# A FiLM layer on one core: loads moved to one queue and cut shorter, stores made longer

## The chip, the cores and the metric

The kernel runs on one core of a Trainium2 chip. The metric is the device time of one execution in microseconds (us), as the median of several runs. A core has a matrix engine (TensorE, PE in the profile), a vector engine (VectorE, DVE), a scalar engine (ScalarE, ACT), a general-purpose vector engine (GpSimd, POOL) and a synchronisation engine (SyncE, SP). They run side by side and wait for one another by semaphores. Data moves between the chip's main memory (DRAM) and the on-chip memory (SBUF, 128 partitions) by 16 DMA engines. A DMA is issued by an engine's instruction queue; here SP and ACT issue them, and each has a queue of its own at every DMA engine (q1 is SP's and q10 is ACT's in this profile). PSUM is the small memory into which TensorE writes.

## The reference

A batch of 32 sequences, each 512 rows of 256 numbers, is scaled and shifted column by column. The scale and the shift depend on the batch entry, and come from two small matrix products. All is float32.

```python
batch, seq, dim = 32, 512, 256      # x: (32, 512, 256); cond_dim = 64
gamma = conditioning @ gamma_proj   # (32, 64) @ (64, 256)
beta = conditioning @ beta_proj
return x * (1 + gamma[:, None, :]) + beta[:, None, :]
```

x is 16.78 MB and so is the output. The small inputs are 8 KB (conditioning) and 64 KB each (the two projections).

## The kernel before, in words

x is cut into four slabs of 8 batch entries (4.19 MB each). In a slab, each of the 128 partitions holds 32 consecutive rows of 256 numbers, which is 32 KB in one piece of DRAM; 16 partitions hold one batch entry. All four slabs have buffers of their own (tiles `xs`), so no load ever waits for a buffer.

**Loads.** SP issues all loads of x at the start (line 59): slab 0 in two DMAs of 8 and 24 rows per partition (runs of 8 and 24 KB), the others in one DMA each (runs of 32 KB). ACT issues the three small loads (lines 48 to 51). A DMA of 128 partitions is dealt out over the 16 DMA engines, 8 partitions to each; a DMA engine moves one run per packet, and adds a small packet that signals completion.

**Preparation.** GpSimd builds a 32 by 32 identity, which VectorE spreads to 32 by 512 (line 67), each column 16 times. One matrix product with it transposes the conditioning and repeats each batch entry 16 times (line 72), so that a column stands for a partition; VectorE copies the result to SBUF (line 74). For each slab a second product (line 79) gives gamma and beta for its 128 partitions, side by side in PSUM (`gb_p`). ScalarE copies them to SBUF (`gb_s`), adding 1 to gamma on the way (lines 82 and 85).

**Work on the slabs.** A slab is worked off in two groups of 16 rows per partition. Of a group VectorE takes 11 rows: it multiplies by (gamma + 1) (line 100) and adds beta (line 103), reading gamma and beta from PSUM. GpSimd takes the other 5 rows with the copies in SBUF (lines 102 and 104). When both are done, ACT issues the store of the group (line 105): 16 rows per partition, runs of 16 KB, 2.1 MB, eight stores in all. The order in which a queue takes its instructions comes from the Tile scheduler's own planning; on GpSimd it came out as two multiplications, then two additions. The scheduler also gives each DMA one of eight semaphores in turn, so a later DMA is issued only when an earlier holder of its semaphore has landed.

Of the kernel before, what the change touches and what calls it, by code (L numbers as in the profile page):

```python
# [2 lines left out]

# [5 lines left out]


@with_exitstack
def kernel(
    ctx: ExitStack,
    tc: tile.TileContext,
    x: bass.AP,
    conditioning: bass.AP,
    gamma_proj: bass.AP,
    beta_proj: bass.AP,
    out: bass.AP,  # L20
):
    nc = tc.nc
    f32 = mybir.dt.float32
    ALU = mybir.AluOpType

    batch, seq, dim = x.shape
    cond_dim = conditioning.shape[1]
    P = 128
    SLABS = 4
    BS = batch // SLABS  # L30
    REP = P // BS
    ROWS = BS * seq // P
    assert SLABS * BS == batch and REP * BS == P and ROWS * REP == seq

    x_v = x.flatten_outer_dims().rearrange("(s p r) d -> s p r d", s=SLABS, p=P)
    o_v = out.flatten_outer_dims().rearrange("(s p r) d -> s p r d", s=SLABS, p=P)

    LOADS = {0: [8, 24]}
    GROUP = 16
    ON_DVE = 11  # L40

    consts = ctx.enter_context(tc.tile_pool(name="consts", bufs=1))
    xpool = ctx.enter_context(tc.tile_pool(name="xpool", bufs=1))
    psum = ctx.enter_context(tc.tile_pool(name="psum", bufs=1, space=bass.MemoryType.PSUM))


    cond_s = consts.tile([batch, cond_dim], f32)
    nc.scalar.dma_start(out=cond_s, in_=conditioning)  # L48
    gbproj = consts.tile([cond_dim, 2 * dim], f32)
    nc.scalar.dma_start(out=gbproj[:, :dim], in_=gamma_proj)  # L50
    nc.scalar.dma_start(out=gbproj[:, dim:], in_=beta_proj)

    slabs = []
    for s in range(SLABS):
        xs = xpool.tile([P, ROWS, dim], f32, name=f"xs{s}")
        slabs.append(xs)
        r = 0
        for n in LOADS.get(s, [ROWS]):
            nc.sync.dma_start(out=xs[:, r : r + n, :], in_=x_v[s, :, r : r + n, :])
            r += n  # L60
        assert r == ROWS


    ident = consts.tile([batch, batch], f32)
    make_identity(nc, ident)
    rident = consts.tile([batch, batch * REP], f32)
    nc.vector.tensor_copy(  # L67
        out=rident.rearrange("p (b g) -> p b g", g=REP),
        in_=ident.to_broadcast([batch, batch, REP]),
    )  # L70
    cond_T_p = psum.tile([cond_dim, batch * REP], f32)
    nc.tensor.matmul(cond_T_p, lhsT=cond_s, rhs=rident, start=True, stop=True)  # L72
    cond_T = consts.tile([cond_dim, batch * REP], f32)
    nc.vector.tensor_copy(out=cond_T, in_=cond_T_p)  # L74

    gb_p, gb_s = [], []
    for s in range(SLABS):
        p_t = psum.tile([P, 2 * dim], f32, name=f"gb_p{s}")
        nc.tensor.matmul(p_t, lhsT=cond_T[:, s * P : (s + 1) * P], rhs=gbproj,  # L79
                         start=True, stop=True)  # L80
        s_t = consts.tile([P, 2 * dim], f32, name=f"gb_s{s}")
        nc.scalar.activation(out=s_t[:, :dim], in_=p_t[:, :dim],  # L82
                             func=mybir.ActivationFunctionType.Identity,
                             bias=1.0, scale=1.0)
        nc.scalar.copy(out=s_t[:, dim:], in_=p_t[:, dim:])  # L85
        gb_p.append(p_t)
        gb_s.append(s_t)

    def rows(t, n):
        return bass.AP(tensor=t.tensor, offset=t.offset, ap=[t.ap[0], [0, n], t.ap[1]])  # L90

    for s in range(SLABS):
        xs = slabs[s]
        g_p, b_p = gb_p[s][:, :dim], gb_p[s][:, dim:]
        g_s, b_s = gb_s[s][:, :dim], gb_s[s][:, dim:]
        for r0 in range(0, ROWS, GROUP):
            v = xs[:, r0 : r0 + ON_DVE, :]
            w = xs[:, r0 + ON_DVE : r0 + GROUP, :]
            nv, nw = ON_DVE, GROUP - ON_DVE
            nc.vector.scalar_tensor_tensor(out=v, in0=rows(g_p, nv), scalar=1.0, in1=v,  # L100
                                           op0=ALU.add, op1=ALU.mult)
            nc.gpsimd.tensor_tensor(out=w, in0=w, in1=rows(g_s, nw), op=ALU.mult)  # L102
            nc.vector.tensor_add(out=v, in0=v, in1=rows(b_p, nv))  # L103
            nc.gpsimd.tensor_tensor(out=w, in0=w, in1=rows(b_s, nw), op=ALU.add)  # L104
            nc.scalar.dma_start(out=o_v[s, :, r0 : r0 + GROUP, :],
                                in_=xs[:, r0 : r0 + GROUP, :])


# [1 line left out]
_INS = ['x', 'conditioning', 'gamma_proj', 'beta_proj']  # L110
_OUTS = [((32, 512, 256), 'float32')]


# [23 lines left out]
```

## Time and profile before

| what | value |
|---|---|
| median of five runs | 84.65 us (84.44 to 84.71) |
| the profiled execution | 84.44 us |
| its span, from first to last instruction | 82.7 us |
| VectorE busy | 49.9 us (60%) |
| GpSimd busy | 46.2 us (56%) |
| TensorE busy | 9.1 us (11%) |
| DMA, both queues | 96.5% of 16 engines' span |
| moved | 33.69 MB, 408 GB/s over the span |
| VectorE works on slabs | from 17.61 to 66.7 us |
| last store issued | 66.77 us |

The span begins with the first instruction of the program and ends with its last; the 1.7 us between it and the execution's time lie outside the program's instructions. The page gives the busy time of each engine, then the span in 40 slices with a digit for tenths, then the DMA queues with the share of 16 engines' time that their packets took. A row of the busy times by stage gives the stretch (start and end in us), its length, the busy time of PE, PEld (weight loads), DVE, ACT and POOL with counts of instructions, TensorE's granted clock (1.00 throughout), the DMA engines' share and GB/s. Packets are counted at their start there, so a short stretch with long packets can show a share above or below what was really used. A row of the timeline gives start, duration, engine, line, operation, the tiles written and read, their shapes, and in brackets the idle time before it and what ended it. A row of the issues gives what is written and read, the queue, how many, KB each, and the median time from issue to landing.

### The profile page before, as it was taken

To read this page: it belongs to the slowest core of one execution; us is meant where nothing else is said; L and a number is where in the kernel's file an instruction comes from. 1 tells how busy PE (TensorE), PEld (TensorE's weight loads), DVE (VectorE), ACT (ScalarE), POOL (GpSimd) and SP (SyncE) were. 2 spreads that over 40 slices of the span, in tenths; PEclk is the share of its full clock that TensorE was granted. 3 is DMA by queue.
4 is the path that set the end of the run, shared out by engine and by line. 5 is a ranking of instruction groups with operands and counts; after the bars stand their busy time and mean duration, and the time that the engine had idled before them with its cause. 6 is when DMAs were issued, how large, how long until landed. Compare 5 with 4: busy or idle time off the path is not lost.

```text
span 82.7 us, 156 instructions
## 1 busy us (share of the span) xinstructions
PE 9.1 (11%) x10; PEld 2.8 (3%) x10; DVE 49.9 (60%) x18; ACT 3.9 (5%) x9; POOL 46.2 (56%) x22
## 2 busy tenths in 40 slices
PE   0090000899600000000000000000000000000000
PEld 0010000443000000000000000000000000000000
DVE  2002000049999999999999999999999920000000
ACT  0600000034400000000000000000000000000000
POOL 2000000059999999999999999999995000000000
DMA  3799999969969989998989969999999999999992
GB/s 56 317 527 396 389 396 523 460 301 507 507 301 460 507 365 381 412 476 381 396 381 523 476 293 476 389 452 436 404 476 389 452 436 404 476 389 452 436 404 103
DMA packets 2080, 33.69 MB, mean 408 GB/s; under 512 B 288, under 2 KB 416, under 8 KB 416
## 3 DMA queue, kind: packets, MB, share of 16 engines
q1 hardware_dynamic: 720, 16.78, 48.6%
q10 hardware_dynamic: 1360, 16.92, 47.9%
HBM read 16.92 MB, written 16.78 MB: 408 GB/s over the span
## 4 chain that ended last, share of the span: by engine, by line
DVE 48%; DMA 16%; issue 11%; PE 2%; ACTq 1%; ACT 1%
DVE xs L100 30%; DVE xs L103 19%; DMA gbproj<-in_beta_proj_dram 16%; PE gb_p L79 2%; ACTq L50 1%; ACTq L48 0%; ACT gb_s L82 0%; ACT gb_s L85 0%
## 5 line engine op out<-in xcount | busy, mean ns | idle before, releaser
L102 POOL TENSOR_TENSOR xs<-xs,gb_s 128x1280 f32<-128x1280 f32 x8 | 23.0, 2887 | 16.3 <-ACT gb_s L82 16.3
L100 DVE SCALAR_TENSOR_TENSOR xs<-gb_p,xs 128x2816 f32<-128x2816 f32 x8 | 24.7, 3085 | 10.9 <-ACT gb_s L85 10.9
L103 DVE TENSOR_TENSOR xs<-xs,gb_p 128x2816 f32<-128x2816 f32 x8 | 24.7, 3087 | 0.3
L104 POOL TENSOR_TENSOR xs<-xs,gb_s 128x1280 f32<-128x1280 f32 x8 | 22.9, 2886 | 0.0
L79 PE MATMUL gb_p<-gbproj,cond_T 64*128 64x512 f32 x8 | 7.2, 1073 | 8.8 <-DMA gbproj<-in_beta_proj_dram 8.8
L74 DVE COPY cond_T<-cond_T_p 64x512 f32<-64x512 f32 x1 | 0.7, 682 | 4.5 <-PE cond_T_p L72 4.5
L79 PEld LDWEIGHTS gb_p<-gbproj,cond_T 64*128 64x128 f32 x8 | 2.5, 326 | 13.6 <-issue 13.6
L72 PE MATMUL cond_T_p<-rident,cond_s 32*64 32x512 f32 x2 | 1.9, 1068 | 4.1 <-DMA cond_s<-in_conditioning_dram 4.1
L82 ACT ACTIVATE gb_s<-gb_p 128x256 f32<-128x256 f32 x4 | 1.5, 384 | 16.5 <-PE gb_p L79 16.5
L85 ACT COPY gb_s<-gb_p 128x256 f32<-128x256 f32 x4 | 1.5, 367 | 0.0
L82 ACT ACT_TABLE_LOAD x1 | 1.3, 1283 | 2.4 <-issue 2.4
L67 DVE COPY rident<-ident 32x512 f32<-32x512 f32 x1 | 0.4, 416 | 1.2 <-POOL ident masks.py:199 1.2
L72 PEld LDWEIGHTS cond_T_p<-rident,cond_s 32*64 32x64 f32 x2 | 0.3, 198 | 4.1 <-issue 4.1
masks.py:197 POOL MEMSET ident<- 32x32 f32 x1 | 0.1, 115 | 0.3 <-POOLq L121 0.3
masks.py:199 POOL TENSOR_SCALAR_AFFINE_SELECT ident<-ident 32x32 f32<-32x32 f32 x1 | 0.2, 202 | 0.1
L121 POOL MEMSET const-float32-0.0<- 128x1 f32 x1 | 0.1, 103 | 0.2 <-issue 0.2
L121 POOL MEMSET const-bfloat16-1.0<- 128x1 bf16 x1 | 0.1, 107 | 0.0
L121 POOL MEMSET const-uint8-127<- 128x1 uint8 x1 | 0.1, 107 | 0.0
L121 POOL MEMSET const-float32-1.0<- 128x1 f32 x1 | 0.1, 103 | 0.0
## 6 DMA issues: line engine op xcount, KB each, us to landing
out_dram<-xs ACTq DMA_DIRECT2D x8, 2048.0 KB, 18.8
xs<-in_x_dram SPq DMA_DIRECT2D x3, 4096.0 KB, 32.9
xs<-in_x_dram SPq DMA_DIRECT2D x1, 3072.0 KB, 12.3
xs<-in_x_dram SPq DMA_DIRECT2D x1, 1024.0 KB, 4.8
gbproj<-in_gamma_proj_dram ACTq DMA_DIRECT2D x1, 64.0 KB, 9.2
gbproj<-in_beta_proj_dram ACTq DMA_DIRECT2D x1, 64.0 KB, 13.0
cond_s<-in_conditioning_dram ACTq DMA_DIRECT2D x1, 8.0 KB, 3.2
```

Of the source, the lines that this page charges most:

```text
L50: nc.scalar.dma_start(out=gbproj[:, :dim], in_=gamma_proj)
L67: nc.vector.tensor_copy(out=rident.rearrange("p (b g) -> p b g", g=REP), in_=ident.to_broadcast([batch, batch, REP]),)
L72: nc.tensor.matmul(cond_T_p, lhsT=cond_s, rhs=rident, start=True, stop=True)
L74: nc.vector.tensor_copy(out=cond_T, in_=cond_T_p)
L79: nc.tensor.matmul(p_t, lhsT=cond_T[:, s * P : (s + 1) * P], rhs=gbproj, start=True, stop=True)
L82: nc.scalar.activation(out=s_t[:, :dim], in_=p_t[:, :dim], func=mybir.ActivationFunctionType.Identity, bias=1.0, scale=1.0)
L85: nc.scalar.copy(out=s_t[:, dim:], in_=p_t[:, dim:])
L100: nc.vector.scalar_tensor_tensor(out=v, in0=rows(g_p, nv), scalar=1.0, in1=v, op0=ALU.add, op1=ALU.mult)
L102: nc.gpsimd.tensor_tensor(out=w, in0=w, in1=rows(g_s, nw), op=ALU.mult)
L103: nc.vector.tensor_add(out=v, in0=v, in1=rows(b_p, nv))
L104: nc.gpsimd.tensor_tensor(out=w, in0=w, in1=rows(b_s, nw), op=ALU.add)
L121: nc = _bacc.Bacc("TRN2", target_bir_lowering=False, num_devices=1)
```

## The change

- All loads go to SP. Slab 0 comes in three DMAs of 8, 8 and 16 rows per partition, then come the three small loads, then slabs 1 to 3 in two DMAs of 16 rows each (runs of 16 KB).
- A slab is still worked off in two pieces of 16 rows, 11 on VectorE and 5 on GpSimd, but it is stored by one DMA for the whole slab: runs of 32 KB, four stores in all. There are 16 DMAs before and after.
- The spread identity (line 67) is gone. The conditioning is transposed with the 32 by 32 identity, and four copies on VectorE, one a slab, repeat its columns 16 times from PSUM.
- The work on the slabs stands in a block whose order is as written (`manual_schedule`): GpSimd multiplies, adds, multiplies, adds.

```diff
-    LOADS = {0: [8, 24]}
-    GROUP = 16
-    ON_DVE = 11
+    SLABS = [(8, [8, 8, 16]), (8, [16, 16]), (8, [16, 16]), (8, [16, 16])]
+    STORES = [[32], [32], [32], [32]]
+    PIECE, ON_DVE = 16, 11
...
+    def load(eng, s, i):
+        sl = slabs[s]
+        r = sum(sl["loads"][:i])
+        n = sl["loads"][i]
+        eng.dma_start(out=sl["xs"][:, r : r + n, :], in_=sl["src"][:, r : r + n, :])
...
-    nc.scalar.dma_start(out=cond_s, in_=conditioning)
-    nc.scalar.dma_start(out=gbproj[:, :dim], in_=gamma_proj)
-    nc.scalar.dma_start(out=gbproj[:, dim:], in_=beta_proj)
...
+    load(nc.sync, 0, 0)
+    load(nc.sync, 0, 1)
+    load(nc.sync, 0, 2)
+    nc.sync.dma_start(out=cond_s, in_=conditioning)
+    nc.sync.dma_start(out=gbproj[:, :dim], in_=gamma_proj)
+    nc.sync.dma_start(out=gbproj[:, dim:], in_=beta_proj)
+    load(nc.sync, 1, 0)
+    load(nc.sync, 1, 1)
...
+    load(nc.sync, 3, 1)
...
-    rident = consts.tile([batch, batch * REP], f32)
-    nc.vector.tensor_copy(
-        out=rident.rearrange("p (b g) -> p b g", g=REP),
-        in_=ident.to_broadcast([batch, batch, REP]),
-    )
-    cond_T_p = psum.tile([cond_dim, batch * REP], f32)
-    nc.tensor.matmul(cond_T_p, lhsT=cond_s, rhs=rident, start=True, stop=True)
-    cond_T = consts.tile([cond_dim, batch * REP], f32)
-    nc.vector.tensor_copy(out=cond_T, in_=cond_T_p)
...
+    cond_T_p = psum.tile([cond_dim, batch], f32)
+    nc.tensor.matmul(cond_T_p, lhsT=cond_s, rhs=ident, start=True, stop=True)
+    for s, sl in enumerate(slabs):
...
+        c_t = consts.tile([cond_dim, P], f32, name=f"cond_T{s}")
+        nc.vector.tensor_copy(
+            out=c_t.rearrange("p (b g) -> p b g", g=rep),
+            in_=cond_T_p[:, b0 : b0 + n].to_broadcast([cond_dim, n, rep]),
+        )
...
+        nc.tensor.matmul(p_t, lhsT=c_t, rhs=gbproj, start=True, stop=True)
...
+    with tc.manual_schedule():
+        for s, sl in enumerate(slabs):
...
+            for n in STORES[s]:
+                for q0 in range(done, done + n, PIECE):
...
+                    nc.vector.scalar_tensor_tensor(out=v, in0=spread(g_p, nv), scalar=1.0, in1=v,
+                                                   op0=ALU.add, op1=ALU.mult)
+                    nc.gpsimd.tensor_tensor(out=w, in0=w, in1=spread(g_s, nw), op=ALU.mult)
+                    nc.vector.tensor_add(out=v, in0=v, in1=spread(b_p, nv))
+                    nc.gpsimd.tensor_tensor(out=w, in0=w, in1=spread(b_s, nw), op=ALU.add)
+                nc.scalar.dma_start(out=sl["dst"][:, done : done + n, :],
+                                    in_=xs[:, done : done + n, :])
+                done += n
```

More of the change, by code (lines that the diff above doesn't have):

```diff
@@ L28 @@
     P = 128
[L29 to L36, printed above, removed]
-    LOADS = {0: [8, 24]}
-    GROUP = 16
-    ON_DVE = 11
+    SLABS = [(8, [8, 8, 16]), (8, [16, 16]), (8, [16, 16]), (8, [16, 16])]
+    assert sum(n for n, _ in SLABS) == batch
+    STORES = [[32], [32], [32], [32]]
+    PIECE, ON_DVE = 16, 11
+    x_f = x.flatten_outer_dims()
+    o_f = out.flatten_outer_dims()
     consts = ctx.enter_context(tc.tile_pool(name="consts", bufs=1))
@@ L44 @@
     psum = ctx.enter_context(tc.tile_pool(name="psum", bufs=1, space=bass.MemoryType.PSUM))
+    slabs = []
+    b0 = 0
+    for s, (n, loads) in enumerate(SLABS):
+        assert P % n == 0
+        rows = n * seq // P
+        r0, r1 = b0 * seq, (b0 + n) * seq
+        slabs.append(dict(
+            n=n, b0=b0, rows=rows, loads=loads,
+            src=x_f[r0:r1, :].rearrange("(p r) d -> p r d", p=P),
+            dst=o_f[r0:r1, :].rearrange("(p r) d -> p r d", p=P),
+            xs=xpool.tile([P, rows, dim], f32, name=f"xs{s}"),
+        ))
+        b0 += n
@@ L47 @@
+    def load(eng, s, i):
[3 more added lines that the diff above has]
+        eng.dma_start(out=sl["xs"][:, r : r + n, :], in_=sl["src"][:, r : r + n, :])
     cond_s = consts.tile([batch, cond_dim], f32)
-    nc.scalar.dma_start(out=cond_s, in_=conditioning)
     gbproj = consts.tile([cond_dim, 2 * dim], f32)
-    nc.scalar.dma_start(out=gbproj[:, :dim], in_=gamma_proj)
-    nc.scalar.dma_start(out=gbproj[:, dim:], in_=beta_proj)
[L53 to L61, printed above, removed]
+    load(nc.sync, 0, 0)
@@ L64 @@
+    load(nc.sync, 0, 1)
[5 more added lines that the diff above has]
+    load(nc.sync, 1, 1)
+    load(nc.sync, 2, 0)
+    load(nc.sync, 2, 1)
+    load(nc.sync, 3, 0)
+    load(nc.sync, 3, 1)
     ident = consts.tile([batch, batch], f32)
     make_identity(nc, ident)
-    rident = consts.tile([batch, batch * REP], f32)
@@ L67 @@
-    nc.vector.tensor_copy(
-        out=rident.rearrange("p (b g) -> p b g", g=REP),
-        in_=ident.to_broadcast([batch, batch, REP]),
-    )
-    cond_T_p = psum.tile([cond_dim, batch * REP], f32)
-    nc.tensor.matmul(cond_T_p, lhsT=cond_s, rhs=rident, start=True, stop=True)
-    cond_T = consts.tile([cond_dim, batch * REP], f32)
-    nc.vector.tensor_copy(out=cond_T, in_=cond_T_p)
-    gb_p, gb_s = [], []
-    for s in range(SLABS):
+    gb_p, gb_s = [], []
+    cond_T_p = psum.tile([cond_dim, batch], f32)
@@ L78 @@
+    nc.tensor.matmul(cond_T_p, lhsT=cond_s, rhs=ident, start=True, stop=True)
+    for s, sl in enumerate(slabs):
+        n, b0 = sl["n"], sl["b0"]
+        rep = P // n
+        c_t = consts.tile([cond_dim, P], f32, name=f"cond_T{s}")
[3 more added lines that the diff above has]
+        )
         p_t = psum.tile([P, 2 * dim], f32, name=f"gb_p{s}")
-        nc.tensor.matmul(p_t, lhsT=cond_T[:, s * P : (s + 1) * P], rhs=gbproj,
-                         start=True, stop=True)
+        nc.tensor.matmul(p_t, lhsT=c_t, rhs=gbproj, start=True, stop=True)
@@ L87, with spread @@
         gb_s.append(s_t)
-    def rows(t, n):
+    def spread(t, n):
         return bass.AP(tensor=t.tensor, offset=t.offset, ap=[t.ap[0], [0, n], t.ap[1]])
[L92 to L106, printed above, removed]
+    with tc.manual_schedule():
+        for s, sl in enumerate(slabs):
+            xs = sl["xs"]
+            g_p, b_p = gb_p[s][:, :dim], gb_p[s][:, dim:]
+            g_s, b_s = gb_s[s][:, :dim], gb_s[s][:, dim:]
+            done = 0
+            for n in STORES[s]:
+                for q0 in range(done, done + n, PIECE):
+                    nv, nw = ON_DVE, PIECE - ON_DVE
+                    v = xs[:, q0 : q0 + nv, :]
+                    w = xs[:, q0 + nv : q0 + PIECE, :]
+                    nc.vector.scalar_tensor_tensor(out=v, in0=spread(g_p, nv), scalar=1.0, in1=v,
[6 more added lines that the diff above has]
+                done += n
+            assert done == sl["rows"]
 _INS = ['x', 'conditioning', 'gamma_proj', 'beta_proj']
```

## The prediction

> **What bounds the kernel now.** I read, in this order: busy shares and slices of the page, the DMA queues, the busy times by stage, the timeline of the vector engine, the issues. The order matters, because the chain of waits alone misleads here: it names VectorE, with 48% of the span.
>
> ```profile
> span 82.7 us, 156 instructions
> ...
> PE 9.1 (11%) x10; PEld 2.8 (3%) x10; DVE 49.9 (60%) x18; ACT 3.9 (5%) x9; POOL 46.2 (56%) x22
> ...
> DMA  3799999969969989998989969999999999999992
> ...
> q1 hardware_dynamic: 720, 16.78, 48.6%
> q10 hardware_dynamic: 1360, 16.92, 47.9%
> ```
>
> VectorE works 60% of the span, the 16 DMA engines 48.6 + 47.9 = 96.5% of it. Queue q1 is SP's (16.78 MB, the loads of x), q10 is ACT's (the eight stores and the three small loads).
>
> ```profile
> 2.00:14.00 12.00, 1.93 (x2) 0.28 (x2) 0.68 (x1) 1.28 (x1) 0.00 (x0) 1.00 1.01 421
> 14.00:28.00 14.00, 7.16 (x8) 2.50 (x8) 10.32 (x4) 2.59 (x8) 10.61 (x4) 1.00 0.99 428
> 28.00:34.00 6.00, 0.00 (x0) 0.00 (x0) 5.96 (x3) 0.00 (x0) 6.00 (x3) 1.00 0.96 377
> 34.00:49.00 15.00, 0.00 (x0) 0.00 (x0) 14.93 (x6) 0.00 (x0) 15.00 (x7) 1.00 1.00 431
> 49.00:67.00 18.00, 0.00 (x0) 0.00 (x0) 17.58 (x6) 0.00 (x0) 14.06 (x5) 1.00 1.01 432
> 67.00:81.00 14.00, 0.00 (x0) 0.00 (x0) 0.00 (x0) 0.00 (x0) 0.00 (x0) 1.00 1.01 431
> ```
>
> The last two columns are the DMA engines' share and GB/s. From 2 to 81 us they never pause; loads alone, loads beside stores and stores alone all run at 421 to 432, but for 377 at 28 to 34 us, when the first store comes in. The compute is finished at 66.7 us; the 14 us after it are stores that had queued up. So the end is start of transfers + their total work + any hole in them. VectorE's 60% costs nothing as long as a store is always waiting.
>
> ```profile
> 17.61 3.09 DVE L100 SCALAR_TENSOR_TENSOR xs<-gb_p,xs 128x2816 f32<-128x2816 f32 x1 [10.86 <-ACT gb_s L85]
> ...
> 63.59 3.09 DVE L103 TENSOR_TENSOR xs<-xs,gb_p 128x2816 f32<-128x2816 f32 x1
> ...
> out_dram<-xs ACTq DMA_DIRECT2D x8, 2048.0 KB, 18.8
> xs<-in_x_dram SPq DMA_DIRECT2D x3, 4096.0 KB, 32.9
> gbproj<-in_beta_proj_dram ACTq DMA_DIRECT2D x1, 64.0 KB, 13.0
> ```
>
> VectorE starts at 17.61, once the small loads and the matmuls behind them are there, and then never waits. A store lands 18.8 us after its issue: that is the backlog.
>
> **The price of the runs.** Medians of the packet records: 8 KB 0.309 us, 16 KB 0.611, 24 KB 0.912, 32 KB 1.213. Each engine carries 8 partitions. Before, per engine: 8 x 0.309 + 8 x 0.912 + 24 x 1.213 + 64 x 0.611 = 78.0 us. After: 16 x 0.309 + 56 x 0.611 + 32 x 1.213 = 78.0. Small loads (0.40) and 16 completions stay. So new run lengths are worth nothing by themselves: shorter loads lose what longer stores win (0.01 us). What is left is order: who waits for what.
>
> The records also show which order the DMA engines take when both queues hold work: one run from one, one from the other, whatever the lengths (32 KB loads against 16 KB stores from 34 to 49 us; 1 KB against 24 KB at 5.7 us). Before, loads got two thirds of the time then, because their runs were twice as long. After the change **stores get two thirds**. This is the step on which the forecast hangs.
>
> [...] The trace switches after each single run. [...]
>
> **Part by part.**
>
> *Small loads to SP, behind slab 0.* Before they alternated on ACT's queue with 24 KB runs; beta landed at 14.72 (issue 1.72 + 13.0). Now they follow 16 runs of 8 KB and 8 of 16 KB on one ring: first packet 1.74 (as before, the same first DMA), + 0.9 (the slowest first packet took 1.19 instead of 0.31) + 4.94 + 4.89 + 0.47 = 12.95, and landing some 0.5 later (slab 0's second DMA: last data 12.87, landed 13.47): beta 13.4, conditioning 13.0. The DMAs of slab 1 are issued three issues later (about 1.3 us at 0.42 each), hidden under 12 us of queued loads. With 12 DMAs on SP, later ones wait for an early one's semaphore, as the fifth did before (issued at 10.42, after gamma); the ring holds over 4 MB then (10 us), so this costs nothing; with an empty ring it would be 1.4 each time, an issue of 0.42 and the 1.0 to the first packet (0.74 to 1.74). ACT loses three issues (1.5 us in sum) at a time when it waits anyway, until 16.9 before.
>
> *Preparation.* Line 67's copy (0.42) goes; it was hidden at the start. Conditioning now arrives with gamma and beta, so its matmul stands on the path: two passes of 32 columns instead of 512 (1.07 each): 0.1 to 0.5 together, I take 0.45 with weight load; then the first of four 64x128 copies, below line 74's 0.68 for 512 columns: 0.3. With hand-overs: 13.0 + 1.0 = 14.0. Then as before two matmul passes (2.06), two ACT copies (0.66): VectorE starts at **16.9**, against 17.61. Bounds 16.3 to 17.5. The other three copies lie on VectorE while PE works.
>
> *Stores of whole slabs.* A slab's four VectorE instructions took 12.34 (17.61 to 29.95), so the first store is issued at 29.3 instead of 26.03. GpSimd's new order (multiply, add, multiply, add) ends before: 4 x 2.89 = 11.6. The first store's packets started 3.70 after issue before; the engine that just missed its turn dates the descriptors' arrival at about 1.14 after issue, the rest is a started 32 KB run and two committed ones. With 16 KB runs that is 1.14 + 0.3 + 1.2 = 2.7: first store run at **32.0**. If the commitment counts bytes, not runs (about 64 to 96 KB), it is 32.6 to 33.8.
>
> *From there by turns.* Loads run from 13.0 to 32.0: 31 runs of 16 KB. Of the 48 of slabs 1 to 3, 17 are left: one of slab 2, all of slab 3. They take 17 turns and three completions; with 20 turns of stores between, of which two are completions, 18 store runs pass. 17 x 0.611 + 18 x 1.213 = 32.2: slab 3's last half lands at 32.0 + 32.2 + 0.5 = **64.7**. Before, the last load landed at 49.6. VectorE wants it at 16.9 + 3.5 x 12.34 = 60.1: **it stands for 4.6 us**. Its first half lands about 50, wanted at 53.9: no wait. Then 6.17 us of work: last store issued at 71.0 (before 66.77), packets from 72.15.
>
> *Is there still cover?* Of the first three stores 24 - 18 = 6 runs are left: 7.3 us, gone at 71.5. So the DMA engines idle some **0.65 us**, then 8 runs of 1.213.
>
> *Sum against the profiled execution* (84.44 = span 82.7 + 1.7 around it): +0.65 idle; -0.25 because small loads no longer break into the big runs (packets 8 to 14 us stretched by 0.25; bounds 0 and -0.25); the slow stretch at 28 to 34 us (6 x (1 - 377/431) = 0.75) I leave as it is: nearest row is the same first store; bounds -0.75 if it belongs to 32 KB loads, +0.75 if mixing, now 32 us long instead of 19, costs it twice. The closing 0.8 us stays. 84.84; against the median 84.65, which lies 0.2 above: **85.0**.
>
> **Rivals.**
> 1. *No hole, faster or equal.* Each 0.61 us by which the first store run comes later takes one load run from the race and 1.2 from the hole. At 32.6 instead of 32.0 it is closed, and the stall of VectorE costs nothing. For it: commitment by bytes; a VectorE start of 17.5. Gamma's first packet, issued at 1.2 and run at 5.66 behind seven 8 KB runs and a 24 KB one, speaks for bytes. Then 84.65 - 0.25 to 84.65: 84.4 to 84.65, or 83.9 without the slow stretch.
> 2. *A bigger hole.* VectorE starts at 16.3: first store 0.6 earlier, hole 0.65 + 1.2 = 1.85; or the last store's descriptors take longer than 1.14 behind a busy engine (3.7 at most, +2.5). 86.2 to 87.
> 3. *Nothing changes* since bytes and DMA count are the same: needs hole and saving to cancel, 84.5 to 84.8.
>
> **How the numbers follow.** Two times of this kernel can be told apart from about 0.2% on (0.17 us). Forecast with a hole of 0.3 to 1.3: 0.43 (84.7 to 85.6); rival 2: 0.16; rival 1 by more than 0.2%: 0.27; rival 3 and the small end of rival 1: 0.14. Slower 0.43 + 0.16 = 0.59. The range leaves out a tenth at each end: 84.1 to 86.6. The forecast's own range is 84.7 to 85.6.
>
> **What would show it.** DMA work in both queues 48 to 49% of a like span (run prices); beta landing about 13.4, VectorE's first big operation at 16.9; first store run near 32.0; in the turns, 16 KB and 32 KB alternating, the last x load landing at 63 to 66; a VectorE wait of 3 to 6 us on a load of x, none before; slices of DMA below 9 near 72 us. If that wait is under 3 us, or the slices stay full, rival 1 holds. If the engines serve several runs of a queue in a row, or share by bytes, the load lands before 60 and the reasoning falls.

## The result: half a per cent slower, and the profile after

The changed kernel takes 85.0 us (median) where the kernel before takes 84.6 in the same comparison: ratio 1.0053, 95% interval 1.0038 to 1.0068. The profiled execution took 85.11 us with a span of 83.3, against 84.44 and 82.7. Its executions also scatter more: most lie between 84.5 and 85.7 us, those of before between 84.4 and 84.7.

From the page of the changed kernel, busy shares, slices and DMA queues (q1 is SP's, q10 is ACT's):

```profile
span 83.3 us, 156 instructions
...
PE 7.6 (9%) x10; PEld 2.8 (3%) x10; DVE 49.8 (60%) x20; ACT 3.9 (5%) x9; POOL 46.6 (56%) x22
...
DMA  2899999999999999999999999999998999899890
...
q1 hardware_dynamic: 1504, 16.92, 49.5%
q10 hardware_dynamic: 576, 16.78, 46.9%
```

The DMA engines are still full to the end: 49.5 + 46.9 = 96.4% of a span that is 0.66 us longer. The digits of 8 near 62, 71 and 77 us come from counting long packets at their start: in the packet records no DMA engine stands still for more than 0.04 us after 34 us. The pause near 72 us that the prediction expected is not there.

Busy times by stage of the changed kernel (the last two columns are the DMA engines' share and GB/s):

```profile
2.00:14.00 12.00, 0.39 (x2) 0.28 (x2) 0.10 (x1) 0.02 (x1) 0.00 (x0) 1.00 1.00 406
...
28.00:34.00 6.00, 0.00 (x0) 0.00 (x0) 5.97 (x3) 0.00 (x0) 5.92 (x3) 1.00 1.04 388
34.00:49.00 15.00, 0.00 (x0) 0.00 (x0) 14.93 (x6) 0.00 (x0) 14.76 (x7) 1.00 1.01 435
49.00:62.00 13.00, 0.00 (x0) 0.00 (x0) 10.91 (x4) 0.00 (x0) 8.53 (x3) 1.00 0.98 418
62.00:67.00 5.00, 0.00 (x0) 0.00 (x0) 3.81 (x2) 0.00 (x0) 3.72 (x2) 1.00 1.00 433
67.00:81.00 14.00, 0.00 (x0) 0.00 (x0) 2.37 (x1) 0.00 (x0) 2.07 (x1) 1.00 1.03 445
```

The slow place at the first store is there again (388 GB/s from 28 to 34 us, 377 before). From 49 to 62 us, where loads and stores still take turns, the rate is 418; before, the stretch from 49 to 67 us held stores alone and ran at 432. Such rates are rough, since a run counts whole in the row where it starts; the packets themselves, below, are exact. VectorE's busy time in that row is 10.91 of 13: it stands.

VectorE's timeline in the changed kernel, and below it the end of the chain of waits:

```profile
17.03 3.09 DVE L118 SCALAR_TENSOR_TENSOR xs<-gb_p,xs 128x2816 f32<-128x2816 f32 x1 [2.25 <-ACT gb_s L100]
...
56.89 3.09 DVE L121 TENSOR_TENSOR xs<-xs,gb_p 128x2816 f32<-128x2816 f32 x1
63.16 3.09 DVE L118 SCALAR_TENSOR_TENSOR xs<-gb_p,xs 128x2816 f32<-128x2816 f32 x1 [3.19 <-DMA xs<-in_x_dram]
66.29 3.09 DVE L121 TENSOR_TENSOR xs<-xs,gb_p 128x2816 f32<-128x2816 f32 x1
```

```profile
13.90 49.23 DMA xs<-in_x_dram
...
63.16 3.10 DVE xs L118
...
66.29 3.09 DVE xs L121
```

The last load was issued at 13.9 and landed at 63.1, after 49 us; before, the last one landed at 49.6. VectorE waits 3.19 us for it, a wait that the kernel before does not have. The last store is issued at 69.45 instead of 66.77. But the store ahead of it keeps the DMA engines busy until 71.7 us on the first of them to finish it, so this lateness does not reach the end in the profiled execution.

Where the 0.66 us are, then, is in the packets. I add up per DMA engine: the work (each run at its median duration: 0.309, 0.611 and 1.213 us for 8, 16 and 32 KB), and the **stretch** (what runs took over that). Work is 78.53 us before and 78.52 after. Stretch is 1.29 before and 1.73 after (+0.45). The 16 DMA engines end their last run between 81.16 and 81.49 before (mean 81.30), and between 81.39 and 82.14 after (mean 81.74); the last one sets the end, 0.19 over the mean before and 0.40 after (+0.21). 0.45 + 0.21 = 0.66. The medians differ by 0.4 us, so this pair of executions shows somewhat more than the typical loss.

### The profile page after: what moved, and what is told of

It reads as the page before. It is cut to its first block, busy times and chain, and to the rows that moved or that the text cites. A ratio compares the mean times of both kernels' runs of the same rounds, so it can differ in the third digit from the quotient of the medians.

```text
span 83.3 us, 156 instructions
## 1 busy us (share of the span) xinstructions
PE 7.6 (9%) x10; PEld 2.8 (3%) x10; DVE 49.8 (60%) x20; ACT 3.9 (5%) x9; POOL 46.6 (56%) x22
## 3 DMA queue, kind: packets, MB, share of 16 engines
q1 hardware_dynamic: 1504, 16.92, 49.5%
q10 hardware_dynamic: 576, 16.78, 46.9%
## 4 chain that ended last, share of the span: by engine, by line
DMA 73%; DVE 7%; SPq 2%; issue 0%
DMA xs<-in_x_dram 73%; DVE xs L118 4%; DVE xs L121 4%; SPq L63 2%
## 5 line engine op out<-in xcount | busy, mean ns | idle before, releaser
L90 DVE COPY cond_T<-cond_T_p 64x128 f32<-64x128 f32 x4 | 0.9, 275 | 13.9 <-PE cond_T_p L85 13.9
## 6 DMA issues: line engine op xcount, KB each, us to landing
gbproj<-in_beta_proj_dram SPq DMA_DIRECT2D x1, 64.0 KB, 10.4
cond_s<-in_conditioning_dram SPq DMA_DIRECT2D x1, 8.0 KB, 11.2
```

Of the source, the lines that this page charges most:

```text
L90: nc.vector.tensor_copy(out=c_t.rearrange("p (b g) -> p b g", g=rep), in_=cond_T_p[:, b0 : b0 + n].to_broadcast([cond_dim, n, rep]),)
```

## The experiments

Two theories stood. **The race**: the DMA engines take runs from SP's and ACT's queue by turns (from 36 to 60 us the changed kernel's packet records have 207 load runs of 16 KB and 217 store runs of 32 KB), so the run lengths decide who gets the time; if the loads lose, VectorE gets its last data late, and if the last store then comes after the others have run out, the DMA engines pause. **The stretch**: no pause; turns between 16 KB loads and 32 KB stores lengthen the runs themselves. A third was that one part alone costs: short loads, long stores, or the place of the small loads. All ratios are to the kernel before, with 95% intervals.

### The changed kernel once more

> The changed kernel once more, unaltered, for a second profile. Hole theory (the DMA engines run dry before the last store): a pause of 0.3 to 1.3 us near 72 us. Stretch theory (no pause; the runs around the first store take longer, 0.8 us per DMA engine instead of 0.54, and the engines end unevenly): no pause, VectorE waits 2 to 5 us for the last load, stretch of all runs 1.6 to 1.9 us per engine, last run ends between 81.7 and 82.3 us; ratio to the kernel before 1.003 to 1.008.

Measured: ratio 1.0040 (1.0013 to 1.0067). VectorE starts at 16.99 and waits 3.3 us at 59.9; no pause; stretch 1.58 us; last runs end between 81.15 and 82.22. So a second profile shows much the same as the first, and the stretch theory's numbers held or nearly so (its stretch lies just under the expected 1.6), while the hole theory's pause is missing again.

The packet records show how the lengthening comes about. They name the queue of a run but not its DMA engine; I set the runs of each engine in a row by their times and by the order of the queues, so which run belongs to which engine is inferred, while the sums over all engines and the ends are read directly. In the first profile the stretch at the first store (30 to 34 us) was 0.81 us per DMA engine on average, in the second 0.66; it was 0.54 before (28 to 34 us). After 36 us twelve of 16 engines lose nothing. The four whose stores began first, at 33.26 to 33.59 us (the others at 33.8 to 34.8), lose 0.46 to 1.02 us each, all on 32 KB stores between 46 and 58 us, and end at 81.89 to 82.14. In the second profile four engines lose about 1.1 us each, most of them among the first to begin; they are the four that end last, 82.18 to 82.22. I call them out of step.

The end does not feel all of that loss, because these engines had lost less than the others at the first store (0.1 to 0.7 us against 0.4 to 1.1). The last of the others ended at 81.96 in the first profile and at 81.80 in the second. So the engines out of step set 0.18 and 0.42 us of the end; the rest of the difference to the kernel before (last end 81.49) is the longer stretch at the first store.

### Half-slab stores again

```diff
-    STORES = [[32], [32], [32], [32]]
+    STORES = [[16, 16], [16, 16], [16, 16], [16, 16]]
```

> The changed kernel with the eight half-slab stores of before (16 KB runs); loads as changed. Race by turns: stores get one half instead of two thirds, the last load lands at 58 to 60 us and VectorE waits for it at most 0.5 us. If the extra stretch belongs to the 32 KB store runs: stretch back to 1.2 to 1.4 us per engine, ratio to the kernel before 0.998 to 1.002. If it belongs to the 16 KB load runs or the small loads behind slab 0: still 1.6 to 1.8, ratio 1.004 to 1.006.

Measured: 1.0066 (1.0044 to 1.0087), with no wait of VectorE; the last load ran until 57.7 us. The stretch is back at 1.36 and the engines end within 0.47 us of each other. I expected the time to come back with it, and it did not. Two terms were missing from the expectation: 16 KB for both loads and stores makes the work 78.85, 0.32 more than before, and the end came 1.42 us after the last run instead of 1.17 (closing waits, explained below). Of the 0.52 us by which the span is longer, 0.19 are in the engines' mean end, 0.08 in the last engine and 0.25 in the closing. So the extra stretch is gone with the 32 KB stores, though the ratio alone would have said the opposite.

### Loads of 32 KB

```diff
-    SLABS = [(8, [8, 8, 16]), (8, [16, 16]), (8, [16, 16]), (8, [16, 16])]
+    SLABS = [(8, [8, 8, 16]), (8, [32]), (8, [32]), (8, [32])]
...
-    load(nc.sync, 1, 1)
...
-    load(nc.sync, 2, 1)
...
-    load(nc.sync, 3, 1)
```

> The changed kernel with slabs 1 to 3 loaded in one DMA each (32 KB runs), stores whole slabs as changed. Race by turns: loads and stores get one half each, last load lands at 51 to 53.5 us, VectorE waits 0 to 0.8 us. Commitment by bytes: the first store runs start 2 to 3 load runs of 32 KB after the descriptors arrive, 33 to 34.5 us, as with 16 KB loads; by number of runs they start 1.5 to 2 us later than in the changed kernel. Stretch owed to 32 KB store runs: 0.8 us at the first store, ratio 1.002 to 1.006; owed to 16 KB loads: 0.5 us, ratio 0.997 to 1.000 (work is 0.2 us less per engine).

Measured: 0.9995 (0.9984 to 1.0006). Last load run ends at 51.0, VectorE never waits, stretch 1.27, engines end between 80.89 and 81.31. So 32 KB stores cost nothing against 32 KB loads. The last engine ended 0.18 us earlier than before, but the end of the span came 1.35 us after it instead of 1.17, which took the gain back.

It also settles what "committed" means. If a store's first run can come 0.85 us after its issue (measured below on idle engines; that it is the same on busy ones is my estimate), a first store found 80 to 96 KB of load runs ahead of it on nearly every engine, the run under way included: three of 32 KB here and before, five or six of 16 KB in the changed kernel. In these three kernels the wait went by bytes, not by runs.

### Small loads first

```diff
-    load(nc.sync, 0, 0)
-    load(nc.sync, 0, 1)
-    load(nc.sync, 0, 2)
     nc.sync.dma_start(out=cond_s, in_=conditioning)
     nc.sync.dma_start(out=gbproj[:, :dim], in_=gamma_proj)
     nc.sync.dma_start(out=gbproj[:, dim:], in_=beta_proj)
+    load(nc.sync, 0, 0)
+    load(nc.sync, 0, 1)
+    load(nc.sync, 0, 2)
```

> The changed kernel with the three small loads at the head of SP's queue, nothing else moved: VectorE starts at about 9 us instead of 17. Race by turns: the stores start earlier (first issued at about 21) and then take two thirds of the DMA time from the loads; VectorE waits three or four times, 10 us or more in sum, last load lands near 66 to 68, the last store is issued at 73 to 75.5 when the others have run out: a pause of 1.8 to 4.2 us, ratio 1.03 to 1.06. If the order of loads and stores doesn't matter: VectorE done at about 60, DMA engines full, ratio 0.998 to 1.005.

Measured: 1.0623 (1.0547 to 1.0699). The compute starts 7 us earlier, and the kernel takes 5 us longer. VectorE's start and its waits for loads after it:

```profile
9.90 3.09 DVE L118 SCALAR_TENSOR_TENSOR xs<-gb_p,xs 128x2816 f32<-128x2816 f32 x1 [6.08 <-DMA xs<-in_x_dram]
...
37.70 3.09 DVE L118 SCALAR_TENSOR_TENSOR xs<-gb_p,xs 128x2816 f32<-128x2816 f32 x1 [3.22 <-DMA xs<-in_x_dram]
...
52.15 3.09 DVE L118 SCALAR_TENSOR_TENSOR xs<-gb_p,xs 128x2816 f32<-128x2816 f32 x1 [8.23 <-DMA xs<-in_x_dram]
...
59.67 3.09 DVE L118 SCALAR_TENSOR_TENSOR xs<-gb_p,xs 128x2816 f32<-128x2816 f32 x1 [1.31 <-DMA xs<-in_x_dram]
...
69.52 3.09 DVE L118 SCALAR_TENSOR_TENSOR xs<-gb_p,xs 128x2816 f32<-128x2816 f32 x1 [3.64 <-DMA xs<-in_x_dram]
```

16.4 us of waits after the start, the last store issued at 75.81, a pause of 3.1 us per DMA engine before it and another 1.1 at the start, where the small loads alone did not fill the engines (4 and 123 GB/s in the first two slices of some 2 us, where the changed kernel has 51 and 346). The race is real, and in this kernel an early start of the compute loses it.

### Small loads on ACT, all else as changed

```diff
+    nc.scalar.dma_start(out=cond_s, in_=conditioning)
+    nc.scalar.dma_start(out=gbproj[:, :dim], in_=gamma_proj)
+    nc.scalar.dma_start(out=gbproj[:, dim:], in_=beta_proj)
     load(nc.sync, 0, 0)
     load(nc.sync, 0, 1)
     load(nc.sync, 0, 2)
-    nc.sync.dma_start(out=cond_s, in_=conditioning)
-    nc.sync.dma_start(out=gbproj[:, :dim], in_=gamma_proj)
-    nc.sync.dma_start(out=gbproj[:, dim:], in_=beta_proj)
```

> The changed kernel with the three small loads issued by ACT at the start, as before the change; all else as changed. They then alternate with runs of 8 and 16 KB instead of standing behind them, so they land 1 to 2 us earlier. Race by turns: VectorE starts at 14.5 to 16.5, the stores 0.5 to 2.5 us earlier, so the last load lands at 62.5 to 67 and VectorE waits 4 us or more; the pause before the last store is 0 to 4 us; ratio 1.005 to 1.04, never below the changed kernel's 1.004. If an earlier start of the compute only helps: ratio 0.998 to 1.003.

Measured: 1.0793 (1.0747 to 1.0839), further than I expected, because the small loads landed sooner: taking turns with runs of 8 and 16 KB beta landed at 9.8 us (1.71 + 8.1), where in the kernel before, beside runs of 8 and 24 KB, it took until 14.7 (1.72 + 13.0), and VectorE started at 12.7. The last load then landed at 71.4, the last store was issued at 77.73, and the DMA engines stood still. VectorE's timeline and the busy times by stage of this kernel:

```profile
12.72 3.09 DVE L118 SCALAR_TENSOR_TENSOR xs<-gb_p,xs 128x2816 f32<-128x2816 f32 x1 [7.35 <-ACT gb_s L100]
...
56.69 3.09 DVE L118 SCALAR_TENSOR_TENSOR xs<-gb_p,xs 128x2816 f32<-128x2816 f32 x1 [7.14 <-DMA xs<-in_x_dram]
...
71.44 3.09 DVE L118 SCALAR_TENSOR_TENSOR xs<-gb_p,xs 128x2816 f32<-128x2816 f32 x1 [8.54 <-DMA xs<-in_x_dram]
```

```profile
49.00:67.00 18.00, 0.00 (x0) 0.00 (x0) 6.73 (x3) 0.00 (x0) 5.78 (x2) 1.00 1.00 429
67.00:72.00 5.00, 0.00 (x0) 0.00 (x0) 0.56 (x1) 0.00 (x0) 0.51 (x1) 1.00 0.92 397
72.00:78.00 6.00, 0.00 (x0) 0.00 (x0) 5.62 (x2) 0.00 (x0) 5.27 (x2) 1.00 0.00 0
78.00:88.00 10.00, 0.00 (x0) 0.00 (x0) 0.00 (x0) 0.00 (x0) 0.00 (x0) 1.00 0.97 419
```

From 72 to 78 us nothing moves while VectorE works on the last half slab: 6.7 us per DMA engine. The first run of the last store begins 0.85 us after its issue, which dates the latency without a queue. So the changed kernel's runs need the small loads behind slab 0: that one part of the change keeps the compute late enough.

### Stores held back

Slab 0's store is issued only after slab 1 is computed, behind two one-column copies on ScalarE that read slab 1:

```diff
+    seen = consts.tile([P, 2], f32)
...
-                nc.scalar.dma_start(out=sl["dst"][:, done : done + n, :],
-                                    in_=xs[:, done : done + n, :])
+                if s > 0:
+                    if s == 1:
+                        nc.scalar.copy(out=seen[:, 0:1], in_=xs[:, ON_DVE - 1, 0:1])
+                        nc.scalar.copy(out=seen[:, 1:2], in_=xs[:, PIECE + ON_DVE - 1, 0:1])
+                        nc.scalar.dma_start(out=slabs[0]["dst"], in_=slabs[0]["xs"])
+                    nc.scalar.dma_start(out=sl["dst"][:, done : done + n, :],
+                                        in_=xs[:, done : done + n, :])
```

> The changed kernel with the first store held back until slab 1 is computed as well (two copies of one column on ScalarE make its queue wait), so that stores begin at about 42 us, when the loads have just ended: no turns at all. If the loss of the changed kernel is the price of turns between 16 KB loads and 32 KB stores (DMA engines out of step): VectorE never waits for a load, no stretch after 36 us, last runs of the 16 engines end within 0.5 us of each other (0.75 and 1.07 in the two profiles of the changed kernel), a pause of 0 to 0.6 us at 42; ratio 0.997 to 1.002. If it is the price of 32 KB stores or of the small loads behind slab 0: still 1.003 to 1.007.

Measured: 1.0019 (0.9995 to 1.0042). VectorE waits for no load. The stretch at the first store, 0.81 us in the changed kernel, is gone; after 36 us every engine loses about 0.27, spread over its runs, none of them more than the others, and all end within 0.17 us (81.72 to 81.89). It pays with a pause of 0.39 us at 42 us, for which the stage's row has 404 GB/s:

```profile
34.00:41.00 7.00, 0.00 (x0) 0.00 (x0) 6.96 (x3) 0.19 (x1) 6.92 (x4) 1.00 0.98 417
41.00:44.00 3.00, 0.00 (x0) 0.00 (x0) 3.00 (x2) 0.19 (x1) 2.92 (x2) 1.00 0.95 404
```

Same runs, same small loads, no turns: no engine out of step. The spread belongs to the turns. The gain over the changed kernel is some 0.3 us (1.0019 against 1.0053); the pause takes about as much again.

### All runs 32 KB

```diff
-    SLABS = [(8, [8, 8, 16]), (8, [16, 16]), (8, [16, 16]), (8, [16, 16])]
+    SLABS = [(8, [32]), (8, [32]), (8, [32]), (8, [32])]
...
-    load(nc.sync, 0, 1)
-    load(nc.sync, 0, 2)
...
-    load(nc.sync, 1, 1)
...
-    load(nc.sync, 2, 1)
...
-    load(nc.sync, 3, 1)
```

> Every load and every store a whole slab in 32 KB runs, small loads behind slab 0 as changed: 4 loads, 4 stores, 3 small. Work per DMA engine 64 x 1.213 + 0.4 = 78.0 us, 0.5 less than before and 0.25 less than the kernel with 32 KB loads for slabs 1 to 3 alone. Turns one to one, DMA engines in step: VectorE starts at about 17, no wait, stretch 1.2 to 1.4, no pause; ratio 0.993 to 0.998. [...]

Measured: 1.0011 (0.9984 to 1.0038): no gain, and my range missed. Work fell to 78.14 as said. But stretch was 1.40, the engines ended unevenly (mean 81.18 against 81.30 before, last 81.51 against 81.49), and from the last landing to the end of the span it was 1.14 us instead of 0.83. About eight engines lose 0.1 to 0.3 us each on 32 KB stores between 41 and 46 us: a smaller loss of the kind that the changed kernel shows, though here all runs are equal. At the end SP waits for the DMA semaphores in a fixed order, one or two to an instruction, some 0.06 us each (in the changed kernel's trace one begins at 63.36, the next at 63.42); the order stands in the program, and here six such instructions were left after the last landing, against one in the kernel before.

### The runs of before, with only the small loads moved and slab 0 cut

```diff
-    SLABS = [(8, [8, 8, 16]), (8, [16, 16]), (8, [16, 16]), (8, [16, 16])]
+    SLABS = [(8, [8, 8, 16]), (8, [32]), (8, [32]), (8, [32])]
...
-    STORES = [[32], [32], [32], [32]]
+    STORES = [[16, 16], [16, 16], [16, 16], [16, 16]]
...
-    load(nc.sync, 1, 1)
...
-    load(nc.sync, 2, 1)
...
-    load(nc.sync, 3, 1)
```

> Slabs 1 to 3 loaded in 32 KB runs, eight stores of 16 KB runs: the run lengths of before, with only the small loads moved behind slab 0 on SP and slab 0 cut in three. Work 78.6, as before. If the move of the small loads costs by itself: ratio 1.002 to 1.006, as the changed kernel. If the loss comes from 16 KB loads against 32 KB stores: 0.998 to 1.002, no VectorE wait, last load at 49 to 51.

Measured: 0.9983 (0.9960 to 1.0006), no wait of VectorE, last load run ended at 49.9, stretch 1.28. The move of the small loads does not cost by itself.

### Whole-slab stores alone, in the kernel before

```diff
-            nc.scalar.dma_start(out=o_v[s, :, r0 : r0 + GROUP, :],
-                                in_=xs[:, r0 : r0 + GROUP, :])
+        nc.scalar.dma_start(out=o_v[s], in_=xs)
```

> The kernel before with one change of the four alone: four whole-slab stores in 32 KB runs instead of eight of 16 KB; loads, queues and preparation as before. Race by turns with equal runs (32 KB against 32 KB): VectorE starts at 17.6, first store issued at 30, last load lands at 51 to 54, VectorE waits at most 0.5 us, no pause, DMA engines in step (last runs end within 0.5 us). Ratio 0.996 to 1.001 (work 0.3 us less per engine). If 32 KB stores are bad by themselves: 1.003 to 1.008.

Measured: 1.0009 (0.9997 to 1.0021). VectorE started at 17.7 and never waited, stretch 1.15, engines ended between 80.66 and 81.20. Long stores alone change nothing.

### 16 KB loads alone, in the kernel before

```diff
-    LOADS = {0: [8, 24]}
+    LOADS = {0: [8, 8, 16], 1: [16, 16], 2: [16, 16], 3: [16, 16]}
```

> The kernel before with 16 KB load runs alone (slab 0 in 8, 8, 16 rows, slabs 1 to 3 in two DMAs each); eight stores of 16 KB, small loads on ACT as before. Small loads alternate with shorter runs, so VectorE starts at 12.5 to 13.5; equal runs take turns one to one: no pause, VectorE waits less than 3 us. Work 78.85, 0.3 us more than before: ratio 1.002 to 1.006. If 16 KB loads lose the race by themselves: a pause and over 1.01.

Measured: 1.0055 (1.0038 to 1.0072). VectorE started at 12.9 and waited 5.0 us at 46 us, longer than I had said, and 0.5 later; no pause. Work 78.85, stretch 1.22. Of the 0.41 us by which the span is longer, 0.14 are in the engines' mean end, 0.03 in the last engine and 0.24 in the closing after it.

### The run with the worst pause, with 32 KB loads

```diff
-    SLABS = [(8, [8, 8, 16]), (8, [16, 16]), (8, [16, 16]), (8, [16, 16])]
+    SLABS = [(8, [8, 8, 16]), (8, [32]), (8, [32]), (8, [32])]
...
-    load(nc.sync, 1, 1)
...
-    load(nc.sync, 2, 1)
...
-    load(nc.sync, 3, 1)
```

on top of the small loads on ACT.

> The kernel of the previous run with the small loads on ACT (which lost 8%), but slabs 1 to 3 loaded in 32 KB runs. VectorE starts as early, at 12.5 to 13. If the pause came from the ratio of the run lengths: turns are now one to one, the last load lands at 54 to 58 instead of 71.4, VectorE waits 3 to 7 us in sum, the last store still arrives with 1 to 4 us of cover, no pause; ratio 0.997 to 1.004. If it came from the early start or from the small loads on ACT: a pause again and over 1.03.

Measured: 1.0030 (1.0010 to 1.0050), where the same kernel with 16 KB loads took 1.0793. VectorE's timeline and one row by stage:

```profile
12.85 3.09 DVE L115 SCALAR_TENSOR_TENSOR xs<-gb_p,xs 128x2816 f32<-128x2816 f32 x1 [7.37 <-ACT gb_s L97]
...
38.25 3.09 DVE L115 SCALAR_TENSOR_TENSOR xs<-gb_p,xs 128x2816 f32<-128x2816 f32 x1 [0.82 <-DMA xs<-in_x_dram]
...
57.82 3.09 DVE L115 SCALAR_TENSOR_TENSOR xs<-gb_p,xs 128x2816 f32<-128x2816 f32 x1 [7.23 <-DMA xs<-in_x_dram]
```

```profile
67.00:81.00 14.00, 0.00 (x0) 0.00 (x0) 3.12 (x2) 0.00 (x0) 2.52 (x1) 1.00 0.97 417
```

VectorE starts as early (12.85) and waits 7.2 us for slab 3 (last load run ended at 56.1), yet the last store was issued at 70.23 and the engines never paused. So the early start alone does not make the pause, and neither do the run lengths alone, since the changed kernel has none: in these runs it took 16 KB loads against 32 KB stores and an early start together.

### The best candidate again

The kernel of the third experiment, unchanged.

> The kernel with 32 KB loads for slabs 1 to 3 and 32 KB stores, small loads behind slab 0, once more with more rounds, as the best candidate: work 78.28 per engine against 78.53 before, DMA engines in step, stretch 1.2 to 1.4: ratio 0.997 to 1.000. If the small gain of work is real, the interval lies below 1.

Measured: 1.0009 (0.9996 to 1.0022), so with the first time (0.9995) no difference to the kernel before. No version here beats the kernel before clearly. Apart from the three with a pause, all of them keep the DMA engines full, and what is left to gain is the stretch at the start, at the small loads and at the first store, some 1.2 us in sum (0.48, 0.25 and 0.54 in the kernel before), of which each variant traded some for something else.

### Side by side

Times per DMA engine in us, from one profile each; "ends" is the first and last DMA engine's end, "closing" the time from the last of these to the end of the span.

| loads / stores, small loads | ratio | work | stretch | pause | ends | closing | longest load wait |
|---|---|---|---|---|---|---|---|
| before: 32 / 16, ACT | 1 | 78.53 | 1.29 | 0 | 81.16 to 81.49 | 1.17 | 0 |
| changed: 16 / 32, behind | 1.0053 | 78.52 | 1.73 | 0 | 81.39 to 82.14 | 1.18 | 3.2 |
| 16 / 16, behind | 1.0066 | 78.85 | 1.36 | 0 | 81.29 to 81.76 | 1.42 | 0 |
| 16 / 16, ACT | 1.0055 | 78.85 | 1.22 | 0 | 81.24 to 81.66 | 1.41 | 5.0 |
| 32 / 32, behind | 0.9995 | 78.28 | 1.27 | 0 | 80.89 to 81.31 | 1.35 | 0 |
| 32 / 16, behind | 0.9983 | 78.61 | 1.28 | 0 | 81.11 to 81.48 | 1.33 | 0 |
| 32 / 32, ACT, slab 0 as before | 1.0009 | 78.21 | 1.15 | 0 | 80.66 to 81.20 | 1.42 | 0 |
| all 32 / 32, behind | 1.0011 | 78.14 | 1.40 | 0 | 80.78 to 81.51 | 1.47 | 0 |
| 16 / 32, stores held back | 1.0019 | 78.52 | 1.39 | 0.4 | 81.72 to 81.89 | 1.17 | 0 |
| 16 / 32, first | 1.0623 | 78.52 | 1.89 | 3.1 | 86.37 to 86.51 | 1.17 | 8.2 |
| 16 / 32, ACT | 1.0793 | 78.52 | 1.47 | 6.7 | 88.30 to 88.44 | 1.18 | 8.5 |
| 32 / 32, ACT | 1.0030 | 78.28 | 1.32 | 0 | 81.02 to 81.56 | 1.33 | 7.2 |

The columns do not add up exactly: the records of neighbouring runs overlap by some 4 ns, so of 0.3 us of work that shorter runs add, about 0.2 shows in the ends.

By the ratio alone, the three kernels in which 16 KB loads take turns without a pause are 0.5 to 0.7% slower, and all with 32 KB loads lie within 0.3% of the kernel before, whatever their stores. The columns show that this is not one cause: with 32 KB stores the loss is stretch and uneven ends, with 16 KB stores it is work and closing.

That the extra stretch belongs to 16 KB loads meeting 32 KB stores rests on all profiles together. In the four where they meet, the stretch at the first store was 0.66 to 1.22 us; in the nine others where a store meets running loads it was 0.03 to 0.60. Two profiles of one kernel differ by up to 0.18, so one pair alone would not have shown it.

## Why the prediction was right in the time and wrong in a step

The time came out at the predicted 85.0, inside the forecast's own range, and slower as forecast. The forecast's mechanism did not: the pause of 0.65 us is not there.

- **The price of the runs** held: 78.53 against 78.52 us of work, no change.
- **Small loads and preparation** held: conditioning landed at 13.3 (2.10 + 11.2), beta at 13.75 (3.35 + 10.4), each 0.3 later than predicted, and VectorE started at 17.03 (predicted 16.9). The first store was issued at 29.44 (29.3). That SP's later DMAs wait for an early one cost nothing, as said: the last was issued at 13.90 and waited 49 us in the queue.
- **By turns** held: 16 KB and 32 KB alternate from 34 to 62 us, and from 36 to 60 us the loads had 33% of the DMA engines' time and the stores 69% (the kernel before, from 34 to 48 us: 128 load runs of 32 KB with 69%, 117 store runs of 16 KB with 32%; a run counts whole where it starts). The last load landed at 63.1 (64.7), VectorE waited 3.2 us (4.6). Two kernels with a pause of 3.1 and 6.7 us, and one in which equal runs took the pause away, show that here the run lengths decided the race.
- **The step that failed is the first store run at 32.0.** I counted what was ahead of it in runs (2.7 us). It is 80 to 96 KB, and these runs were themselves stretched by 0.8 us, so the store's runs began at 33.26 to 34.76. That is rival 1's condition, named there at 32.6: 13 to 15 load runs were left instead of 17, the last store was issued at 69.45 instead of 71.0, and with 0.85 us to its first run (1.14 predicted) it came 1.4 us before the first DMA engine ran out (71.70). What would have told me was in the packet records of before: gamma's first packet waited behind some 80 KB of short runs, and I gave it to the rival.
- **Two terms that I left at nothing took the pause's place.** The slow stretch at the first store, bounds -0.75 and +0.75, I took as unchanged: it grew by 0.27 (0.12 in the second profile). Four engines out of step later on added 0.17 to the mean, and 0.21 more to the last one. And the 0.25 that I took off for undisturbed big runs was not saved: the small loads in a burst stretched the runs at 12 to 14 us by 0.24. So 0.65 - 0.25 = 0.40 predicted against 0.27 + 0.17 + 0.21 = 0.65 measured in the profiles. The sum was near by luck; rival 1's price (84.4 to 84.65) lacked these terms.

Open: only two executions of the changed kernel were profiled, and neither has a pause. Most of its unprofiled times lie below 85.7 us, but four reach 85.9 to 87.8; whether a pause occurs in those, with a cover of 1.1 to 1.4 us in the two profiles, isn't shown. Why stores on an engine that is out of step take longer was not tried either; shown is only that held-back stores end it. Smaller losses of the kind, 0.1 to 0.3 us an engine and on 32 KB runs, stand in four other kernels: on one engine of the kernel before, on three of each kernel with 32 KB loads and stores whose small loads are on ACT, and on eight of the one with all runs of 32 KB. None stands in the other profiles without a pause. Nor was it tried why the first store stretches the loads more when 16 KB loads meet 32 KB stores.

## What to carry to other kernels

Two queues fed the same DMA engines here, and while both had work the one with the longer runs had about two thirds of the time (69% for 32 KB against 16 KB, in both directions: with 32 KB loads against 16 KB stores the last load landed at 49.6 us, the other way round at 63.1). For a kernel whose records show such turns: give the longer runs to the queue whose data something waits for, or make them equal. In this kernel, whose DMA engines are busy for 96% of the span, an earlier compute was slower by 6 and 8% in two runs, since its stores then crowded out loads; what has to be watched is whether the last store arrives before the others have drained. Judge such a change by the packets' work, their lengthening, the pauses and the last engine's end, each by itself: a ratio near 1 hid opposite terms here in several runs.

## What the runs showed of the hardware that I had not expected

- The first store, coming to busy engines, started behind some 80 to 96 KB of already committed load runs per engine, the run under way included, on nearly every engine of the kernel before, the changed one and the one with 32 KB loads: 2.9 to 4.5 us in the first two, an estimate that gives it the same 0.85 us from issue as was measured on idle engines. In the two kernels with 32 KB loads and stores whose small loads are on ACT it was 128 KB on 6 and 10 of the 16 engines.
- The first store lengthened the load runs around it: 0.54 us per DMA engine in sum in the kernel before, 0.81 and 0.66 in the two profiles of the changed one, 0.2 to 1.2 in the others; in the kernel with all runs of 32 KB it was 0.03, and where the first store came only after the loads had ended it was not there. Why was not found.
- In both profiles of the changed kernel, where 16 KB loads meet 32 KB stores, four of the 16 DMA engines fell out of step and lost 0.46 to some 1.1 us each, of which 0.18 and 0.42 us showed at the end; with other run lengths such losses were 0.3 us or less.
- SP's closing waits took about 0.06 us for each wait instruction that is left when the last store has landed: one in the kernel before, six in the kernel with all runs of 32 KB, 0.3 us of a possible gain of 0.4.
